# Second half of an RMSNorm: all eight multiplications moved to VectorE, read from the PSUM bank of the scale

## The chip, the cores and the metric

The kernel runs on one core of a Trainium2 chip. The time is device microseconds of one execution. Before the change it is 2491.94 us, the median of three runs (2489.65 to 2494.43). One further execution was profiled; all rows of the trace come from it. Engine names are those of the profile: PE is TensorE (PEld its weight loads), DVE is VectorE, ACT is ScalarE, POOL is GpSimd, SP the engine that issues the DMAs of the weights.

## What is computed

The reference is a trunk of two layers; x is 512 tokens by 1024 features in fp32. Each layer has three sub-layers, an FFN, a mixer and a second FFN, and every one begins with the same step:

```
def rms_norm(x, gain):
    xf = x.astype(jnp.float32)
    y = xf * lax.rsqrt(jnp.mean(xf * xf, axis=-1, keepdims=True) + EPS)
    return (y * gain.astype(jnp.float32)).astype(x.dtype)

h = modulate(rms_norm(x, norm_gain[l, i]), shift, scale)      # h * (1 + scale) + shift
x = x + 0.5 * gate * swiglu(h, w_gate, w_up, w_down)          # FFN
x = x + gate * hybrid_mixer(h, ...)                           # mixer
```

The norm at the head of a sub-layer stands between two stretches of matrix products: it needs the whole x that the last product of the sub-layer before it completes, and the first product of the next sub-layer needs its result h. There are six norms. The first is written apart, at the start of the program; the other five, at the seams between sub-layers, go through the class `Norm`, and the change is in that class alone.

## The kernel before

**Layout and precision.** x is kept transposed, features on the 128 partitions and tokens along the free axis, in eight slices d = 0 to 7 of 128 features, two slices to a tile. Products are made to fp32 precision from three matmuls: each operand is split into a high part and a low part (`hi`, the value rounded to fp32r, and `lo`, the rest), and lines 119, 120 and 121 multiply high by high and the two mixed pairs. So h exists as `hhi` and `hlo`, 8 slices of 128x512 each.

**The norm in two halves of tokens.** At a seam everything goes in two halves of 256 tokens (`hs` = 0 and 1), so that the first products on half 0 can run while half 1 is still being normalised. For a half there are these steps:
- `sq`, as each slice of x is completed (line 425 on DVE adds the product of the sub-layer before): ACT squares it (L314, for the last slice L319), POOL adds the square to `ssum` (L315; for the last slice DVE, L320, into the tile `strip`), and ACT writes the slice scaled by gain and 1 + scale into a tile `xa` (L323).
- `front`: PE adds the squares over the partitions (L332), DVE makes the inverse square root by Newton steps on 128x2 numbers (L334, L276, L282 to L284) and writes it on the diagonal of a 128x128 matrix, twice (L337, into `strip`).
- `back_start`: PE multiplies ones by the diagonals (L351). This leaves the scale of each token, repeated on all partitions, in a PSUM bank `rb` of 128x256. ACT copies the bank to the third part of `strip` (L353).
- eight pieces, one per slice d: a multiplication t = xa * scale, on DVE from the PSUM bank for d = 0, 3 and 6 (L360) and on POOL from the copy for d = 1, 2, 4, 5 and 7 (L362); then ACT adds the shift and rounds to `hhi` (L364), and DVE makes `hlo` = t + shift - hhi (L365).

**What consumes it.** In an FFN, PE takes slice after slice d: three matmuls of 256 tokens for the gate (`pg`) and three for the up projection (`pu`), then, for all eight slices, 24 for a second gate unit (`pg1`). In the mixer it takes six matmuls of 512 columns per slice, for the first six slices, out of weights fetched ahead (`ptb`, `b`). Half 1 follows in the same way.

**What sets the order.** Each engine carries out its own list of instructions in order and waits on semaphores for the others. The lists come from a scheduler in the tile library, which reorders what the program emits; the program itself delays pieces by a counter of matmuls (`later`, `poll`, `STEP`). The weights are loaded by SP, rounded to high parts on ACT (L268) and split on DVE (L270), well ahead of PE. `strip` is a tag with two buffers. PSUM has two tags of four banks, `mm` and `acc`; `rb` takes one of them in turn.

Of the kernel before, what the change touches and what calls it, by code (L numbers as in the profile page):

```python
# [15 lines left out]
F32 = mybir.dt.float32  # L16
# [3 lines left out]
ALU = mybir.AluOpType  # L20
AX = mybir.AxisListType

P = 128
# [17 lines left out]
def encoder_kernel(tc, xT, c, w_ada, b_ada, gains, w_gate, w_up, w_down, w_qkv, w_f, w_ubg,  # L41
                   qk_gain, rel, fbias, w_pool, pool_scale, w_branch, w_out, inv_cnt, w_first, out):
    nc = tc.nc
# [16 lines left out]
    def nm(s):  # L60
        uid[0] += 1
        return f"{s}_{uid[0]}"

    def st(shape, dt, tag, bufs):
        return sb.tile(shape, dt, tag=tag, bufs=bufs, name=nm(tag))
# [7 lines left out]
    def blk(tag, dt=F32R):  # L73
        bufs = {"xv": 4, "v2": 4, "b": NB}[tag]
        return st([P, 2, T], dt, tag, bufs)

    def t1(cols=T):
        return st([P, cols], F32, "t1", 2)
# [19 lines left out]
    def later(delay, fn, group=None):  # L98
        t = Task(pe[0] + delay, fn, group)
        tasks.append(t)  # L100
        return t
# [33 lines left out]
    for b in range(4):  # L135
        xb = blk("xv", F32)
        nc.sync.dma_start(xb, xT[:, 2 * b:2 * b + 2, :])
        x_blocks.append(xb)
        sq = st([P, 2, T], F32, "wlo" if b else "whi", 3)
        for a in range(2):  # L140
            nc.scalar.activation(sq[:, a, :], xb[:, a, :], AF.Square)
        squares.append(sq)
        if b < 2:
            pc = mmt()
            mm(pc, ones[0:1, :], crow[:, b * T:(b + 1) * T], start=True, stop=True)
            crows.append(pc)
# [141 lines left out]
    def xd(d):  # L288
        return x_blocks[d // 2][:, d % 2, :]

    HALF = T // 2


    class Norm:
# [10 lines left out]
        def sq(self, d, hs):  # L305

            cols = slice(0, T) if hs is None else slice(hs * HALF, (hs + 1) * HALF)
            x = xd(d)[:, cols]
            n = cols.stop - cols.start
            if d == 0:  # L310
                nc.scalar.activation(self.ssum[:, cols], x, AF.Square)
            elif d < KD - 1:
                q = t1(T)[:, :n]
                nc.scalar.activation(q, x, AF.Square)  # L314
                nc.gpsimd.tensor_tensor(self.ssum[:, cols], self.ssum[:, cols], q, op=ALU.add)  # L315
            else:
                self.work[hs] = st([P, 3 * HALF], F32, "strip", 2)
                w = self.work[hs][:, :HALF]
                nc.scalar.activation(w, x, AF.Square)  # L319
                nc.vector.tensor_tensor(w, w, self.ssum[:, cols], op=ALU.add)  # L320
            if d % 2 == 0 and self.xa[d // 2] is None:
                self.xa[d // 2] = blk(self.xtag, F32)
            nc.scalar.activation(self.xa[d // 2][:, d % 2, cols], x, AF.Identity, scale=apre[:, self.l, self.s, d:d + 1])  # L323
# [20 lines left out]
        def back_start(self, hs, bank):  # L344
            if self.state[hs] > 1:
                return
            self.front(hs, bank)
            self.state[hs] = 2
            w = self.work[hs]
            rb = bank((P, HALF))  # L350
            mm(rb, ones, w[:, HALF:2 * HALF], start=True, stop=True)  # L351
            rbs = w[:, 2 * HALF:3 * HALF]
            nc.scalar.copy(rbs, rb)  # L353
            cols = slice(hs * HALF, (hs + 1) * HALF)

            def piece(d):
                b = modc[:, self.l, 3 * self.s, d:d + 1]
                t = self.xa[d // 2][:, d % 2, cols]
                if d in ON_DVE:
                    nc.vector.tensor_tensor(t, rb, t, op=ALU.mult)  # L360
                else:
                    nc.gpsimd.tensor_tensor(t, rbs, t, op=ALU.mult)  # L362
                hi = hhi[:, d, cols]
                a_ins = nc.scalar.activation(hi, t, AF.Identity, bias=b)  # L364
                v_ins = nc.vector.scalar_tensor_tensor(hlo[:, d, cols], t, b, hi.bitcast(F32),  # L365
                                                       op0=ALU.add, op1=ALU.subtract)
                gate["scalar"], gate["vector"] = a_ins.ins, v_ins.ins
                last["norm"] = v_ins.ins

            self.pieces[hs] = [lambda d=d: piece(d) for d in range(KD)]  # L370
            for d in range(KD):
                later(STEP * d, lambda d=d: self.pieces[hs].pop(0)() if len(self.pieces[hs]) == KD - d else None)
# [59 lines left out]
    FRONT, BACK, FRONT1, BACK1 = 8, 24, 16, 28  # L432
    FRONT2, BACK2 = 16, 28
    STEP = 3
    ON_DVE = (0, 3, 6)


    class Ffn:
# [205 lines left out]
    def proj_qk(l, col, gcol, is_q, res, pre=None, norm=None):  # L644
# [3 lines left out]
        def evac(t, a):  # L648
            if t == 0:
                qs.extend((st([P, NT, T], F32, "ptb", 2), st([P, NT, H], F32, "qss", 1)))  # L650
            qn, ss = qs
            nc.scalar.copy(qn[:, t, :], a)
            sq = t2(T)
            nc.scalar.activation(sq, a, AF.Square)  # L654
            nc.vector.tensor_reduce(ss[:, t, :], sq.rearrange("p (h d) -> p h d", h=H), axis=AX.X, op=ALU.add)
# [441 lines left out]
```

## Time and profile before

| | before |
|---|---|
| median of 3 runs | 2491.94 us (2489.65 to 2494.43) |
| the profiled execution | 2496.94 us, its span in the trace 2495.0 us |
| PE busy | 2429.8 us, 97% of the span, 11898 matmuls |
| DVE busy | 1378.6 us, 55% |
| ACT busy | 983.6 us, 39% |
| POOL busy | 380.7 us, 15% |
| the copy of the scale (L353) | 10 times, 373 ns median |
| multiplications on DVE from PSUM (L360) | 30, medians 414 to 416 ns |
| multiplications on POOL from the copy (L362) | 50, medians 741 and 914 ns |

The row of a timeline gives the start in us, the duration in us (of all instructions of the row together, where it ends in xN), engine, line, operation, out<-in and shape, and in brackets the idle time of the engine just before and what ended it. Matmuls are pipelined, so a row's duration is longer than the distance to the next row; the distance is what PE needs for one. PEclk in a row of stretches is the TensorE clock that was granted, 1.00 being full speed.

### The profile page before, as it was taken

The numbers are of one execution on the slowest core, as the hardware profiler recorded it, in microseconds if no ns is written. First come the engines' busy times: TensorE is split into PE (matmuls) and PEld (weight loads), VectorE is DVE, ScalarE is ACT, GpSimd is POOL, SyncE is SP. The second block draws the span as 40 slices with busy tenths as digits, with TensorE's granted clock in tenths as the row PEclk, the third lists the DMA queues.
The fourth block names the chain that finished last, engine by engine and source line by source line (L and its number), as shares of the span: only waits on it lengthen the run. The fifth ranks groups of instructions, "written<-read, shape, count | busy, mean of one in ns | idle before, by whom it ended". The sixth has DMA issues, their size and how long they took to land. (4 is left out here: it accounts for less than half of the span.)

```text
span 2495.0 us, 30866 instructions
## 1 busy us (share of the span) xinstructions
PE 2429.8 (97%) x11898; PEld 2030.3 (81%) x11898; DVE 1378.6 (55%) x2424; ACT 983.6 (39%) x1644; POOL 380.7 (15%) x377
## 2 busy tenths in 40 slices
PE   7999999989999999999999999999999999999999
PEld 5888888767788898888888888977777888888888
DVE  8655536788753465555365543467787434533332
ACT  5322235677532442223333222356765334422231
POOL 2000003343322220000110000124332322100000
PEclk9999999999999999999999999999999999999999
DMA  7655542223323425555335533323233233232322
GB/s 276 224 186 199 180 141 80 85 72 96 104 89 110 146 99 193 178 207 181 119 114 191 190 114 99 126 78 92 67 105 99 93 115 130 69 101 93 102 93 93
DMA packets 116263, 320.02 MB, mean 128 GB/s; under 512 B 11122, under 2 KB 13298, under 8 KB 116116
## 3 DMA queue, kind: packets, MB, share of 16 engines
q1 hardware_dynamic: 114962, 313.86, 37.3%
q0 software_dynamic: 1152, 4.19, 0.4%
q8 instruction: 93, 1.52, 0.2%
q14 instruction: 54, 0.44, 0.1%
q10 hardware_dynamic: 2, 0.00, 0.0%
HBM read 311.64 MB, written 6.38 MB: 127 GB/s over the span
## 5 line engine op out<-in xcount | busy, mean ns | idle before, releaser
L268 ACT CAST whi<-raw 128x1024 fp32r<-128x1024 f32 (+1 forms) x395 | 411.8, 1046 | 1090.9 <-PE acc L120 416.7
L270 DVE TENSOR_TENSOR wlo<-raw,whi 128x1024 fp32r<-128x1024 f32 x339 | 419.1, 1239 | 519.5 <-ACT whi L268 507.5
L121 PE MATMUL mm<-hhi,wlo 128*128 128x512 f32 x1304 | 507.4, 389 | 0.4 <-DVE wlo L270 0.4
L119 PE MATMUL mm<-hhi,whi 128*128 128x512 f32 x1304 | 507.6, 389 | 0.0
L120 PE MATMUL mm<-hlo,whi 128*128 128x512 f32 x1304 | 507.3, 389 | 0.0
L119 PE MATMUL acc<-b,whi 128*128 128x512 f32 (+1 forms) x960 | 355.9, 371 | 0.0
L121 PE MATMUL acc<-b,wlo 128*128 128x512 f32 (+1 forms) x960 | 353.4, 368 | 0.0
L120 PE MATMUL acc<-b,whi 128*128 128x512 f32 (+1 forms) x960 | 353.4, 368 | 0.0
L121 PEld LDWEIGHTS mm<-hhi,wlo 128*128 128x128 f32 x1304 | 244.7, 188 | 51.5 <-DVE wlo L270 0.9
L119 PEld LDWEIGHTS mm<-hhi,whi 128*128 128x128 f32 x1304 | 245.1, 188 | 50.8
L120 PEld LDWEIGHTS mm<-hlo,whi 128*128 128x128 f32 x1304 | 244.8, 188 | 50.9
L197 DVE CUSTOM_DVE_ANT_0 v<-v,b,badac 128x1024 f32<-128x1024 f32 x144 | 189.3, 1316 | 40.3 <-DMA v<-in_w_ada_dram 40.0
L121 PEld LDWEIGHTS acc<-b,wlo 128*128 128x128 f32 x960 | 180.9, 188 | 29.6
L120 PEld LDWEIGHTS acc<-b,whi 128*128 128x128 f32 x960 | 181.0, 189 | 29.3 <-DVE b L376 0.3
L119 PEld LDWEIGHTS acc<-b,whi 128*128 128x128 f32 x960 | 181.0, 189 | 28.8
L119 PE MATMUL acc<-hhi,whi 128*128 128x512 f32 x480 | 191.7, 401 | 1.7 <-ACT hhi L564 1.7
L120 PE MATMUL acc<-hlo,whi 128*128 128x512 f32 x480 | 188.5, 393 | 1.1 <-DVE hlo L567 1.1
L121 PE MATMUL acc<-hhi,wlo 128*128 128x512 f32 x480 | 188.9, 393 | 0.5 <-POOL wlo L270 0.4
L462 DVE TENSOR_TENSOR t<-mm,t 128x512 f32<-128x512 f32 x86 | 59.5, 691 | 210.0 <-PE mm L121 205.9
L270 POOL TENSOR_TENSOR wlo<-raw,whi 128x1024 fp32r<-128x1024 f32 (+1 forms) x56 | 132.5, 2370 | 172.1 <-ACT whi L268 137.3
L119 PE MATMUL acc<-whi,hhi 128*128 128x512 f32 x336 | 137.6, 409 | 4.9 <-ACT t L654 3.7
L120 PE MATMUL acc<-wlo,hhi 128*128 128x512 f32 x336 | 131.8, 392 | 0.0
(235 smaller groups left out, 3473.3 us busy)
## 6 DMA issues: line engine op xcount, KB each, us to landing
v<-in_w_ada_dram SPq DMA_DIRECT2D x144, 512.0 KB, 4.5
raw<-in_w_down_dram SPq DMA_DIRECT2D x88, 512.0 KB, 3.7
raw<-in_w_up_dram SPq DMA_DIRECT2D x82, 512.0 KB, 3.5
raw<-in_w_gate_dram SPq DMA_DIRECT2D x79, 512.0 KB, 3.5
raw<-in_w_ubg_dram SPq DMA_DIRECT2D x56, 512.0 KB, 3.5
raw<-in_w_qkv_dram SPq DMA_DIRECT2D x42, 512.0 KB, 3.6
raw<-in_w_branch_dram SPq DMA_DIRECT2D x24, 512.0 KB, 3.7
raw<-in_w_out_dram SPq DMA_DIRECT2D x16, 512.0 KB, 3.6
```

The lines of the kernel that those rows point to most:

```text
L119: mm(o, lh, rh, start=start, stop=False)
L120: mm(o, lh, rl, start=False, stop=False)
L121: mm(o, ll, rh, start=False, stop=stop)
L197: dot = nc.vector.tensor_tensor_reduce(out=raw, in0=raw, in1=silc[0], scale=1.0, scalar=badac[:, l, j, d:d + 1], op0=ALU.mult, op1=ALU.add ...
L268: nc.scalar.copy(hi, raw)
L270: lo_eng.tensor_tensor(lo, raw, hi.bitcast(F32), op=ALU.subtract)
L462: nc.vector.tensor_tensor(pr, pu, sg, op=ALU.mult)
```

## The change

The multiplication of every piece goes to DVE and reads the scale from its PSUM bank. The copy of the bank on ACT and the third part of `strip` go away; POOL has no part in the second half of the norm any more. The bank `rb` is read until the multiplication of piece 7, where before it was last read by the copy and the pieces 0, 3 and 6.

```
@@ Norm.sq
-                self.work[hs] = st([P, 3 * HALF], F32, "strip", 2)
+                self.work[hs] = st([P, 2 * HALF], F32, "strip", 2)
@@ Norm.back_start
             mm(rb, ones, w[:, HALF:2 * HALF], start=True, stop=True)
-            rbs = w[:, 2 * HALF:3 * HALF]
-            nc.scalar.copy(rbs, rb)
             cols = slice(hs * HALF, (hs + 1) * HALF)

             def piece(d):
                 b = modc[:, self.l, 3 * self.s, d:d + 1]
                 t = self.xa[d // 2][:, d % 2, cols]
-                if d in ON_DVE:
-                    nc.vector.tensor_tensor(t, rb, t, op=ALU.mult)
-                else:
-                    nc.gpsimd.tensor_tensor(t, rbs, t, op=ALU.mult)
+                nc.vector.tensor_tensor(t, rb, t, op=ALU.mult)
                 hi = hhi[:, d, cols]
                 a_ins = nc.scalar.activation(hi, t, AF.Identity, bias=b)
@@
     STEP = 3
-    ON_DVE = (0, 3, 6)
```

The changed program is six lines shorter, so its lines are renumbered: L360 (multiplication) becomes L357, L364 (`hhi`) L359, L365 (`hlo`) L360, L376 L371, L425 L420. The scheduler also sets the lists differently at the five seams. Three places matter.

**DVE, half 0 of the norm ahead of the first mixer.** `v_422` is the tile of slices 0 and 1, `v_425` of 2 and 3, `v_458` of 4 and 5, `v_461` of 6 and 7; `mm_2871` is the bank of the scale. Before:

```order
L360 TENSOR_TENSOR v_422_2488<-mm_2871,v_422_2488 128x256 [waits Activation_49]
L360 TENSOR_TENSOR v_425_2523<-mm_2871,v_425_2523 128x256
L360 TENSOR_TENSOR v_461_2767<-mm_2871,v_461_2767 128x256
L365 SCALAR_TENSOR_TENSOR hlo<-v_422_2488,modc,hhi 128x256 [waits Activation_49]
L425 SCALAR_TENSOR_TENSOR xv_97<-acc_2548,modc,xv_97 128x256 [waits PE_49]
L365 SCALAR_TENSOR_TENSOR hlo<-v_425_2523,modc,hhi 128x256 [waits Activation_49]
```

Now:

```order
L357 TENSOR_TENSOR v_422_2488<-mm_2871,v_422_2488 128x256 [waits PE_49]
L357 TENSOR_TENSOR v_422_2488<-mm_2871,v_422_2488 128x256
L357 TENSOR_TENSOR v_425_2523<-mm_2871,v_425_2523 128x256 x2
L360 SCALAR_TENSOR_TENSOR hlo<-v_422_2488,modc,hhi 128x256 [waits Activation_49] x2
L420 SCALAR_TENSOR_TENSOR xv_97<-acc_2548,modc,xv_97 128x256 [waits PE_49]
L360 SCALAR_TENSOR_TENSOR hlo<-v_425_2523,modc,hhi 128x256 [waits Activation_49] x2
L420 SCALAR_TENSOR_TENSOR xv_97<-acc_2549,modc,xv_97 128x256 [waits PE_49]
L357 TENSOR_TENSOR v_458_2732<-mm_2871,v_458_2732 128x256 x2
```

The first multiplication waits for PE instead of the copy on ACT, and four multiplications stand ahead of the first `hlo` where three stood.

**ACT, half 1 of the same norm.** Before, with the copy of the scale first:

```order
L353 COPY strip_2916<-mm_2997 128x256 [waits PE_49]
L364 ACTIVATE hhi<-v_422_2488,modc 128x256 [waits Pool_49]
L364 ACTIVATE hhi<-v_422_2488,modc 128x256 [waits DVE_49]
L364 ACTIVATE hhi<-v_425_2523,modc 128x256 [waits Pool_49]
L364 ACTIVATE hhi<-v_425_2523,modc 128x256 [waits DVE_49]
```

Now:

```order
L359 ACTIVATE hhi<-v_422_2488,modc 128x256 [waits DVE_49] x2
L359 ACTIVATE hhi<-v_425_2523,modc 128x256 [waits DVE_49] x2
L359 ACTIVATE hhi<-v_458_2732,modc 128x256 [waits DVE_49] x2
L359 ACTIVATE hhi<-v_461_2767,modc 128x256 [waits DVE_49] x2
```

Before, slice 1, which POOL multiplies, was rounded ahead of slice 0; now the slices go in their order.

**DVE, the inverse square root of half 1, same norm.** Before, all of half 0's `hlo` stood ahead of L334, the first step of it. Now one multiplication and one `hlo` (slice 7 of half 0) stand around and inside it:

```order
L357 TENSOR_TENSOR v_461_2767<-mm_2871,v_461_2767 128x256
L334 TENSOR_SCALAR nt_v_2960<-mm_2957 128x2 [waits PE_49]
L371 TENSOR_TENSOR ssum_4753<-wf_4751,ssum_4753 128x8x8 [waits Activation_49]
L276 TENSOR_SCALAR nt_j_2962<-nt_v_2960 128x2 [waits DVE_49]
L282 TENSOR_TENSOR nt_q_2964<-nt_j_2962 128x2 [waits DVE_49]
L283 SCALAR_TENSOR_TENSOR nt_u_2965<-nt_q_2964,nt_v_2960 128x2 [waits DVE_49]
L360 SCALAR_TENSOR_TENSOR hlo<-v_461_2767,modc,hhi 128x256 [waits Activation_49]
L284 SCALAR_TENSOR_TENSOR nt_z_2966<-nt_u_2965,nt_j_2962 128x2 [waits DVE_49]
```

The other four seams have the same pattern (without L371 in the FFNs). In PE's list L351 of half 1 moves back by one matmul at the mixers and by two at the FFNs, where L332 of half 1 moves ahead by seven.

More of the change, by code (lines that the diff above doesn't have):

```diff
@@ L316, in sq @@
             else:
-                self.work[hs] = st([P, 3 * HALF], F32, "strip", 2)
+                self.work[hs] = st([P, 2 * HALF], F32, "strip", 2)
                 w = self.work[hs][:, :HALF]
@@ L351, in back_start @@
             mm(rb, ones, w[:, HALF:2 * HALF], start=True, stop=True)
-            rbs = w[:, 2 * HALF:3 * HALF]
-            nc.scalar.copy(rbs, rb)
             cols = slice(hs * HALF, (hs + 1) * HALF)
@@ L358, in piece @@
                 t = self.xa[d // 2][:, d % 2, cols]
[L359 to L362, printed above, removed]
+                nc.vector.tensor_tensor(t, rb, t, op=ALU.mult)
                 hi = hhi[:, d, cols]
@@ L434, in encoder_kernel @@
     STEP = 3
-    ON_DVE = (0, 3, 6)
     class Ffn:
```

## The prediction

> **What bounds the kernel now.** I read the page first, then the stretches, the waits of PE, and the timeline of each seam.
>
> ```profile
> span 2495.0 us, 30866 instructions
> PE 2429.8 (97%) x11898; PEld 2030.3 (81%) x11898; DVE 1378.6 (55%) x2424; ACT 983.6 (39%) x1644; POOL 380.7 (15%) x377
> PE acc L121 <- DVE hlo L365: 4.3, 2, 2.2
> PE acc L119 <- ACT hhi L364: 1.7, 2, 0.8
> PE mm L119 <- ACT hhi L364: 1.3, 3, 0.4
> PE mm L120 <- DVE hlo L365: 1.1, 3, 0.4
> PE acc L332 <- DVE strip L320: 0.7, 3, 0.2
> ```
>
> PE bounds the program, so a change in the norm is worth what it takes from PE at the five seams, and nothing else. The waits (us in total, times, longest) that PE has on the norm's second half come to 4.3 + 1.7 + 1.3 + 1.1 + 0.7 = 9.1 us, two at each mixer seam and three at each FFN seam. They are not the whole loss. The timeline of PE at the first mixer:
>
> ```profile
> 387.40 0.40 PE L119 MATMUL acc<-ptb,hhi 128*128 128x512 f32 x1
> 387.63 0.40 PE L120 MATMUL acc<-ptb,hhi 128*128 128x512 f32 x1
> 390.19 0.61 PE L121 MATMUL acc<-ptb,hlo 128*128 128x512 f32 x1 [2.16 <-DVE hlo L365]
> 390.59 0.63 PE L119 MATMUL acc<-ptb,hhi 128*128 128x512 f32 x1
> 393.94 0.39 PE L121 MATMUL acc<-ptb,hlo 128*128 128x512 f32 x1
> 394.16 0.39 PE L119 MATMUL acc<-ptb,hhi 128*128 128x512 f32 x1
> 395.56 0.50 PE L332 MATMUL mm<-ones,strip 128*128 128x1 f32 x4
> 398.79 0.70 PE L351 MATMUL mm<-strip,ones 128*128 128x256 f32 x2
> 400.48 0.40 PE L121 MATMUL acc<-b,hlo 128*128 128x512 f32 x1
> 401.71 0.50 PE L119 MATMUL acc<-ptb,hhi 128*128 128x512 f32 x1 [0.83 <-ACT hhi L364]
> 390.19:393.94 3.75, 3.75 (x10) 2.96 (x10) 3.69 (x10) 3.27 (x9) 1.77 (x4) 0.54 0.49 156
> ```
>
> An unhindered matmul of 512 columns follows the one before it after 0.23 us. From 387.63 to 390.19 it took 2.56: 2.33 lost. Then nine matmuls took 3.75 us where 9 x 0.23 = 2.1 were due, and the last row (a stretch; the third number from its end is the granted clock) says why: the clock stood at 0.54. That is 1.6 more, of which I count 1.5. Half 1 loses 401.71 - 400.48 - 0.23 = 1.0, and 0.1 in the matmul after it. So a first mixer seam loses 3.8 in half 0 and 1.1 in half 1. The second mixer seam has the same two waits and, read in the same way, loses 4.0 and 1.1:
>
> ```profile
> 1625.07 0.50 PE L121 MATMUL acc<-ptb,hlo 128*128 128x512 f32 x1 [2.16 <-DVE hlo L365]
> 1636.60 0.50 PE L119 MATMUL acc<-ptb,hhi 128*128 128x512 f32 x1 [0.83 <-ACT hhi L364]
> ```
>
> Together 10.0 us.
>
> What made `hlo` late there, on DVE, POOL and ACT:
>
> ```profile
> 385.13 1.09 DVE L360 TENSOR_TENSOR v<-mm,v 128x256 f32<-128x256 f32 x3 [0.35 <-ACT strip L353]
> 386.25 3.88 DVE L365 SCALAR_TENSOR_TENSOR hlo<-v,modc,hhi 128x256 fp32r<-128x256 f32 x1
> 386.38 3.46 POOL L362 TENSOR_TENSOR v<-strip,v 128x256 f32<-128x256 f32 x5
> 393.00 1.28 DVE L365 SCALAR_TENSOR_TENSOR hlo<-v,modc,hhi 128x256 fp32r<-128x256 f32 x3
> 399.93 1.09 DVE L360 TENSOR_TENSOR v<-mm,v 128x256 f32<-128x256 f32 x3 [1.20 <-ACT strip L353]
> 401.29 4.71 DVE L365 SCALAR_TENSOR_TENSOR hlo<-v,modc,hhi 128x256 fp32r<-128x256 f32 x8 [0.28 <-ACT hhi L364]
> 399.98 4.15 POOL L362 TENSOR_TENSOR v<-strip,v 128x256 f32<-128x256 f32 x5 [6.54 <-ACT strip L353]
> 384.73 0.37 ACT L353 COPY strip<-mm 128x256 f32<-128x256 f32 x1 [0.17 <-PE mm L351]
> 399.52 0.37 ACT L353 COPY strip<-mm 128x256 f32<-128x256 f32 x1 [5.63 <-PE mm L351]
> 400.75 2.17 ACT L364 ACTIVATE hhi<-v,modc 128x256 fp32r<-128x256 f32 x5 [0.85 <-POOL v L362]
> ```
>
> One `hlo`, an operation with both tensors in SBUF, lasted 3.88 us; POOL's five multiplications ran from 386.38 to 389.84, and DVE came free 0.3 us behind them. Three `hlo` with POOL quiet (393.00) take 1.28, so 0.48 one and 0.40 from one to the next. Beside POOL's multiplications (401.29) eight take 4.71, 0.6 from one to the next. The multiplications on DVE, which read one tensor from PSUM, keep 0.34 from one to the next beside POOL. So POOL's multiplications hold up DVE's `hlo`, but not DVE's multiplications. The Trainium skill, page "SBUF — State Buffer", section "Who interferes with whom", states just that: an instruction of DVE with two SBUF inputs contends with one of GpSimd that reads SBUF, the one that starts first blocking the other, and one with at most one SBUF input does not. By that rule the new multiplications are free of it and the old contention ends; the rows agree.
>
> The third thing in these rows: in half 1 ACT waits for POOL (400.75), whose product of slice 1 stands in ACT's list ahead of slice 0. PE's first `hhi` is the second one ACT writes.
>
> An FFN seam, whose units of work on PE are 0.12 us (256 columns):
>
> ```profile
> 891.35 0.28 PE L119 MATMUL mm<-hhi,ptb 128*128 128x256 f32 x1
> ...
> 895.56 0.28 PE L121 MATMUL mm<-hhi,ptb 128*128 128x256 f32 x1
> 896.06 0.61 PE L332 MATMUL acc<-ones,strip 128*128 128x1 f32 x4 [0.22 <-DVE strip L320]
> 899.46 0.64 PE L351 MATMUL acc<-strip,ones 128*128 128x256 f32 x2
> 901.60 0.28 PE L121 MATMUL mm<-hhi,b 128*128 128x256 f32 x1
> 902.32 0.50 PE L119 MATMUL mm<-hhi,ptb 128*128 128x256 f32 x2 [0.44 <-ACT hhi L364]
> 902.66 0.28 PE L119 MATMUL mm<-hhi,b 128*128 128x256 f32 x1
> 903.32 0.38 PE L120 MATMUL mm<-hlo,ptb 128*128 128x256 f32 x1 [0.38 <-DVE hlo L365]
> 903.55 0.28 PE L121 MATMUL mm<-hhi,ptb 128*128 128x256 f32 x1
> ```
>
> Half 0 loses 896.06 - 895.56 - 0.12 = 0.4 at L332 and, ahead of it, some 0.4 in five delays of about 0.1 at `hlo` (read one by one from the timeline). Half 1: from 901.60 to 903.55 five matmuls took 1.95 where 5 x 0.12 = 0.6 were due, 1.35. In all 2.15; the two other FFN seams read the same. Three times 2.15 is 6.5, so the most that can be won is 10.0 + 6.5 = 16.5 us.
>
> **The change part by part.**
>
> The copy: 10 times 0.37 off ACT. It stood on the path of every half: DVE began 0.40 behind ACT's start (399.93 against 399.52, 385.13 against 384.73), so a half's first product comes 0.4 earlier, 0.7 behind the start of L351.
>
> The five multiplications a half that move: POOL loses 50 of about 0.8; DVE gains 50 x 0.34 = 17 us. DVE's share of the program does not matter (55%); its list within a seam does. A piece now costs DVE 0.34 + 0.40 = 0.74 and ACT 0.40 to 0.45. PE needs six matmuls a slice: 1.40 us at a mixer, 0.71 at an FFN. So a mixer is safe, and at an FFN DVE is 0.03 slower a slice, 0.2 in a half, within the lead that it has there.
>
> *Mixer, half 0.* In the written order, with the times of the old rows: first multiplications at 384.73, 385.07, 385.40, 385.74; ACT rounds slice 0 from 385.6 to 386.1 (the two older instructions L314 and L323 first); `hlo` 0 at 386.2, or 386.4 if POOL's one sum (L315) holds it, 1 at 386.8, then a residual (L425, 0.4), 2 and 3 by 388.5, the next residual, then slices 4 and 5 with `hlo` at 390.3 to 391.1. PE asks for `hlo` d at 387.86 + 1.40 d, so for 4 at 393.5. Nothing is late. The 3.8 (4.0) goes, the slow clock with it, since the gap ahead of it goes.
>
> *Mixer, half 1.* Here the change adds a wait. Before, L351 began 3.23 us behind L332, just as DVE's chain ended. Now an `hlo` (0.40) stands in the chain, and PE has one more matmul (0.23): a new wait of 0.2, up to 0.4 if L371 also takes a place. Behind L351 come five matmuls, until 1.7 us behind its start; slice 0 is multiplied at 0.7, rounded from 1.25 to 1.75. A wait of 0.1 in place of 1.0. Half 1 keeps 0.3 to 0.5 of its 1.1: I take 0.5. Gain of a mixer seam 3.8 + 0.6 = 4.4 (4.6 the second): 9.0 us.
>
> *FFN, half 0.* In the same way `hlo` 4, the first behind both residuals, is done at about 894.5. PE begins slice 0 at 891.35 and, 24 matmuls on, slice 4 at 894.2; L332 is now ahead of `hlo` 4 in PE's list, at 894.4, with its input (L320) done by 893.6, so PE asks for `hlo` 4 at 895.1. `hlo` 7, inside the inverse root, ends at 896.7, asked for at 897.3. The chain has 33 matmuls of cover (3.9 us and 0.5 for L332 itself) where 24 stood, and needs 3.4 + 0.4: no wait. The 0.8 goes, or 0.1 stays.
>
> *FFN, half 1.* 13 matmuls stay behind L351, so PE asks for slice 0 at 2.0 us behind its start and has it at 1.75; for `hlo` 0 at 2.25, there at 2.3; `hlo` 6 is within 0.1. About 0.2 stays of 1.35. Gain of an FFN seam 1.9, three times 5.7.
>
> Nothing else pays. `rb` is held some 6 us longer, but the next tile that takes its bank comes a unit of work later. The splits of weights that follow (L270) begin up to 1 us later relative to PE; the first of them is needed 11.4 us behind L351 and is there by 9.
>
> Sum: 9.0 + 5.7 = 14.7 us, of at most 16.5. The profiled execution goes from a span of 2495.0 to 2480.3; it took 2496.94, 1.9 around the span and 5.0 over the median. The median 2491.94 goes to 2477.2; I say 2478, with a wait or two overlooked.
>
> **Unknown costs.** A DVE list with two multiplications between `hlo`s is not in the trace. From below it keeps the 0.34 and 0.40; from above `hlo` keeps the 0.6 of row 401.29 for another reason than POOL. I take the first, by row 393.00, which differs from it in POOL alone. The wait at L351 lies between 0 and 0.4 at a mixer. Whether PE's gain passes through to the end: PE's list of waits names no DMA, so what follows moves with PE; at worst it is all absorbed.
>
> **The rivals.**
>
> *Only the mixers win (2483).* The FFN seams run on units of 0.71 a slice with a lead of a few tenths; if DVE's order makes one `hlo` late in each half, waits of the old size come back. Against it, the order above. 9.0 us remain.
>
> *The long `hlo` stays (2486).* If 3.88 us were not POOL's doing, the mixers would win 0.6 each and the FFNs as forecast, 6 us in all. Against it: its end follows POOL's fifth multiplication.
>
> *Absorbed (2492).* PE comes early at the end of a seam and waits for something that does not move. For it: attention between the seams has PE waits of its own. Against it: they are on DVE and ACT, which are fed by PE.
>
> *Slower: DVE becomes the bound of the FFN halves (2498).* If `hlo` stays at 0.6 from one to the next, a piece costs 0.94 against PE's 0.71: 8 x 0.23 = 1.8 a half, 11 in six halves. If each FFN seam also brings one slow spell of the clock (1.5, as at 390.19), 4.5 more. The FFNs' old loss of 6.5 stays; less the mixers' 9.0 the time grows by 6.5. It decides from an `hlo` distance of 0.56 on (48 x 0.19 = 9.0). Against it: row 393.00. The Trainium skill, page "TensorE: Matmul & The Clock Gate", section "What's actually happening", puts the half clock behind an idle window of about 3.4 us; the row at 390.19 has it behind 2.16 us of idle already, so the row decides. By the page, short waits at the FFNs would bring no slow spell and this rival would end at 2494.
>
> **How the numbers follow.** Forecast 0.62, only the mixers 0.17, long `hlo` stays 0.06, absorbed 0.09, slower 0.06. The forecast's own range is 2474 to 2482: from the whole 16.5 and a lower draw (the three runs lie within 2.5 of their median) to 11 us of gain with a higher one. To hold 8 in 10 it is carried on over the first rival and its spread: 2473 to 2486. A measurement tells about 0.2%, 5 us, from no change. Faster than 2487: the first two, the most of the third: 0.83. Within 0.2%: absorbed and the rest of the third, 0.11. Slower 0.06.
>
> **What would show it.** No `hlo` over 1 us; eight in half 1 of a seam 0.40 apart; full clock at both mixer seams; PE without a wait over 0.5 there; ACT's first `hhi` of half 1 1.25 behind L351 instead of 1.96; a small wait of PE at L351 of the mixers' half 1. It is wrong if PE's wait on `hlo` appears at later slices of the FFN halves, if `hlo` stays long, or if the seams get shorter and the span does not.

## The result and the profile after

The changed kernel takes 2479.69 us, the median of five runs (2475.76 to 2481.9), where the kernel before, in five runs beside it, takes 2491.94. The ratio is 0.9948 with a 95% interval of 0.9937 to 0.996, so 10 to 16 us are won. Its profiled execution took 2480.69 us. The page of it begins:

```profile
span 2478.9 us, 30855 instructions
PE 2425.1 (98%) x11898; PEld 2030.1 (82%) x11898; DVE 1372.2 (55%) x2474; ACT 979.9 (40%) x1634; POOL 340.5 (14%) x327
```

POOL has 50 instructions fewer and DVE 50 more, and yet DVE is busy 6 us less: the multiplications add 17 us (50 x 0.34), the `hlo` that no longer wait beside POOL take 18 away (53.4 us busy before, 35.0 now), and the rest of the 6 lies outside the norm. Of the five rows of PE's waits that were shown of before (9.1 us in all), none is left in the list of after: no entry names `hlo` or `hhi` of the norm (L360, L359), or `strip` from L320.

The first mixer seam in the timeline of after, on PE, DVE and ACT (start, duration, then as before; multiplication is now L357, `hhi` L359, `hlo` L360):

```profile
388.66 0.40 PE L120 MATMUL acc<-ptb,hhi 128*128 128x512 f32 x1
388.89 0.39 PE L121 MATMUL acc<-ptb,hlo 128*128 128x512 f32 x1
...
392.63 0.50 PE L332 MATMUL mm<-ones,strip 128*128 128x1 f32 x4
...
396.14 0.70 PE L351 MATMUL mm<-strip,ones 128*128 128x256 f32 x2
...
397.59 0.39 PE L121 MATMUL acc<-b,hlo 128*128 128x512 f32 x1
397.89 0.50 PE L119 MATMUL acc<-ptb,hhi 128*128 128x512 f32 x1
385.75 1.42 DVE L357 TENSOR_TENSOR v<-mm,v 128x256 f32<-128x256 f32 x4
387.15 0.98 DVE L360 SCALAR_TENSOR_TENSOR hlo<-v,modc,hhi 128x256 fp32r<-128x256 f32 x2
...
396.87 1.08 DVE L357 TENSOR_TENSOR v<-mm,v 128x256 f32<-128x256 f32 x3 [0.79 <-PE mm L351]
397.88 1.29 DVE L360 SCALAR_TENSOR_TENSOR hlo<-v,modc,hhi 128x256 fp32r<-128x256 f32 x3
399.08 1.08 DVE L357 TENSOR_TENSOR v<-mm,v 128x256 f32<-128x256 f32 x3
397.33 1.31 ACT L359 ACTIVATE hhi<-v,modc 128x256 fp32r<-128x256 f32 x3 [4.16 <-DVE v L357]
```

PE goes from L120 to the first `hlo` product in 0.23 us where it needed 2.56. Two `hlo` take 0.98 in half 0 instead of 3.88 for one. In half 1, DVE does three multiplications, three `hlo`, three multiplications: 399.08 - 396.87 = 2.21 for three pieces, 0.74 a piece. ACT's first `hhi` starts 1.19 behind L351 (1.96 before), and PE's first product of half 1 comes 0.30 behind the matmul ahead of it, 0.07 more than it needs. The stretch that held the slow clock before now reads (third number from the end is the granted clock):

```profile
388.40:391.40 3.00, 3.00 (x15) 2.45 (x14) 3.00 (x9) 2.47 (x7) 1.75 (x4) 1.00 0.31 127
```

The first FFN seam, on PE:

```profile
891.04 0.40 PE L119 MATMUL mm<-hhi,ptb 128*128 128x256 f32 x2
891.27 0.50 PE L332 MATMUL acc<-ones,strip 128*128 128x1 f32 x4
...
895.63 0.59 PE L351 MATMUL acc<-strip,ones 128*128 128x256 f32 x2
...
897.49 0.28 PE L121 MATMUL mm<-hhi,b 128*128 128x256 f32 x1
897.61 0.40 PE L119 MATMUL mm<-hhi,ptb 128*128 128x256 f32 x2
897.84 0.35 PE L120 MATMUL mm<-hlo,ptb 128*128 128x256 f32 x1
898.03 0.28 PE L121 MATMUL mm<-hhi,ptb 128*128 128x256 f32 x1
```

L332 no longer waits, and half 1 begins 0.12 behind the last matmul of half 0, the distance that a matmul of 256 columns needs.

For all kernels below I use one measure, the length of a seam on PE: from L351 of half 0 to the first matmul with weights behind the seam that are not fetched ahead. PE has the same matmuls in it in all of them, so a difference is time that PE lost.

| kernel | mixer seams, us | FFN seams, us | sum of five | against after | median, us | ratio to the runs of before beside it (95%) |
|---|---|---|---|---|---|---|
| before | 26.12, 26.12 | 23.57, 23.58, 23.56 | 122.95 | +16.6 | 2491.94 | 1 |
| after | 21.21, 21.21 | 21.33, 21.33, 21.29 | 106.37 | 0 | 2479.69 | 0.9948 (0.9937 to 0.996) |
| before, again | 26.14, 24.59 | 23.58, 23.57, 23.59 | 121.47 | +15.1 | 2493.26 | 1.0001 (0.9992 to 1.0009) |
| before, a third time | 26.14, 24.60 | 23.58, 23.60, 23.59 | 121.51 | +15.1 | 2491.18, one run | |
| after, again | 21.23, 21.22 | 21.33, 21.33, 21.30 | 106.41 | 0 | 2479.07 | 0.9943 (0.9931 to 0.9956) |
| after, POOL reads | 23.41, 23.41 | 22.69, 22.70, 22.70 | 114.91 | +8.5 | 2490.26 | 0.9986 (0.9977 to 0.9995) |
| after, POOL writes | 21.30, 21.29 | 21.33, 21.33, 21.33 | 106.58 | +0.2 | 2478.35 | 0.9953 (0.9936 to 0.997) |
| after, a copy nobody reads | 21.94, 21.94 | 21.96, 21.94, 21.95 | 109.73 | +3.4 | 2482.84 | 0.9959 (0.9947 to 0.9972) |
| after, DVE reads the copy | 22.02, 22.03 | 22.66, 22.66, 22.66 | 112.03 | +5.7 | 2484.99 | 0.9968 (0.9955 to 0.998) |
| before, two slices on POOL | 23.14, 23.12 | 22.97, 22.93, 22.94 | 115.10 | +8.7 | 2487.27 | 0.9977 (0.9968 to 0.9986) |
| after, every product twice | 24.42, 24.41 | 25.31, 25.61, 25.61 | 125.36 | +19.0 | 2500.56 | 1.0034 (1.0021 to 1.0047) |

The stretches of the FFNs between the seams are 341.9 us in all these traces; those with attention lie between 475.0 and 479.4 from one execution to the next, whichever kernel runs. That is why one profile can be some us off its median.

### The profile page after: what moved, and what is told of

Read it like the earlier page. It is cut to its first block, busy times and chain, and to the rows that moved or that the text cites. A ratio compares the mean times of both kernels' runs of the same rounds, so it can differ in the third digit from the quotient of the medians.

```text
span 2478.9 us, 30855 instructions
## 1 busy us (share of the span) xinstructions
PE 2425.1 (98%) x11898; PEld 2030.1 (82%) x11898; DVE 1372.2 (55%) x2474; ACT 979.9 (40%) x1634; POOL 340.5 (14%) x327
## 3 DMA queue, kind: packets, MB, share of 16 engines
q8 instruction: 93, 1.52, 0.3%
## 5 line engine op out<-in xcount | busy, mean ns | idle before, releaser
L120 PE MATMUL mm<-hlo,whi 128*128 128x512 f32 x1304 | 507.3, 389 | 0.0
L120 PE MATMUL acc<-b,whi 128*128 128x512 f32 (+1 forms) x960 | 353.4, 368 | 0.0
L120 PEld LDWEIGHTS mm<-hlo,whi 128*128 128x128 f32 x1304 | 244.8, 188 | 50.8
L120 PEld LDWEIGHTS acc<-b,whi 128*128 128x128 f32 x960 | 181.1, 189 | 29.3 <-DVE b L371 0.3
L120 PE MATMUL acc<-hlo,whi 128*128 128x512 f32 x480 | 188.9, 394 | 1.0 <-DVE hlo L561 1.0
L120 PE MATMUL acc<-wlo,hhi 128*128 128x512 f32 x336 | 132.3, 394 | 0.0
```

The source lines that it names most:

```text
L120: mm(o, lh, rl, start=False, stop=False)
```

## Experiments

My theory: the gain is the end of POOL's reading of SBUF beside DVE's `hlo`, plus the copy (0.4 on the path of each half) and ACT's list, which no longer puts POOL's product first. The rivals: the gain comes from the copy, or from the other order of the lists that the scheduler sets, or POOL is late for its own sake and PE waits for its products.

### POOL reads SBUF, and nobody waits for it

In the changed kernel, behind the multiplication of slice 0 of each half, POOL gets five products that no instruction reads. The norm is computed as in the changed kernel, and PE's matmuls stand in the same order.

```
                nc.vector.tensor_tensor(t, rb, t, op=ALU.mult)
+               if d == 0:
+                   for o in (w[:, 2 * HALF:], w[:, :HALF], w[:, HALF:2 * HALF], self.ssum[:, cols], w[:, 2 * HALF:]):
+                       nc.gpsimd.tensor_tensor(o, t, t, op=ALU.mult)
```

> The changed kernel with five extra multiplications on GpSimd in each half, t * t of slice 0 into memory that nobody reads, so that GpSimd is as busy at that place as before but nobody waits for its products; the lists of PE, DVE and ACT are those of the changed kernel but for a few rows. Theory 1a (contention: GpSimd's reads of SBUF hold up DVE's hlo): hlo lasts 2 to 4 us once in half 0 of each mixer seam, hlo of half 1 are 0.6 apart, the seams lose 2 to 5 us each at the mixers and 1 to 2 at the FFNs, time 2487 to 2492. Theory 1b (only the lateness and the order of GpSimd's products mattered): hlo stays at 0.48 us, the time stays at 2480.

Measured: 2490.26 us, ratio 0.9986 (0.9977 to 0.9995); the seams are 8.5 us longer than in after. The first mixer seam, in the timeline of this kernel (the products that nobody reads are L360, `hlo` is L363):

```profile
385.91 3.81 DVE L363 SCALAR_TENSOR_TENSOR hlo<-v,modc,hhi 128x256 fp32r<-128x256 f32 x2
386.15 1.75 POOL L360 TENSOR_TENSOR strip<-v 128x256 f32<-128x256 f32 x3
387.87 0.60 POOL L360 TENSOR_TENSOR ssum<-v 128x256 f32<-128x256 f32 x1
388.44 0.60 POOL L360 TENSOR_TENSOR strip<-v 128x256 f32<-128x256 f32 x1
389.38 0.50 PE L121 MATMUL acc<-ptb,hlo 128*128 128x512 f32 x1 [1.57 <-DVE hlo L363]
398.33 2.20 POOL L360 TENSOR_TENSOR strip<-v 128x256 f32<-128x256 f32 x3 [5.97 <-DVE v L357]
398.83 1.99 DVE L363 SCALAR_TENSOR_TENSOR hlo<-v,modc,hhi 128x256 fp32r<-128x256 f32 x3
```

The old picture is back with work that nobody waits for. The row of two `hlo` takes 3.81 us; less 0.40 for the second, the first one lasts 3.4, until 0.3 behind the end of POOL's fifth product at 389.04, and PE waits. In half 1 three `hlo` take 1.99 instead of 1.29. So POOL's reading alone takes back more than half of the seams' gain (8.5 of 15.1 to 16.6) and three quarters of the medians' (by the ratios 0.0014 is left of 0.0055), with the copy gone and the products of the norm all on DVE. Behind this shorter wait the clock stayed whole:

```profile
389.00:394.00 5.00, 4.62 (x22) 3.85 (x23) 5.00 (x14) 2.84 (x7) 1.60 (x4) 1.00 0.42 155
```

PE's list is that of after, matmul for matmul; ACT's and DVE's differ from it in the place of one instruction at each mixer seam. So if the parts simply add up, the rivals "the copy" and "the lists" cannot be more than the rest; "POOL late for its own sake" has no share in these 8.5 us.

### POOL as an engine that only writes

The same place, but twelve memsets in place of the five products.

```
+               if d == 0:
+                   for i in range(3):
+                       for o in (w[:, HALF:2 * HALF], w[:, :HALF], self.ssum[:, cols], w[:, 2 * HALF:]):
+                           nc.gpsimd.memset(o, 0.0)
```

> The changed kernel, and in each half, behind the multiplication of slice 0, POOL gets twelve memsets of 128x256 that nobody reads: POOL is as long busy as with the five products of the run before it, about 3.5 us a half, but only writes SBUF and reads nothing. The computation is whole. Theory (what holds hlo up is that POOL reads SBUF while DVE reads two tensors from SBUF): hlo stays at 0.40 from one to the next, no wait of PE on hlo at the mixers, the seams sum to 106.4 to 107.5 us, and the time is that of the changed kernel, 2479 to 2481. Rival (any work of POOL beside hlo, or POOL's writes to SBUF, holds it up): hlo of several us in the mixers' half 0 as with the five products, seams near 115, time 2488 to 2491. A third, between: memsets hold only the hlo that meets the write of one of them, then hlo 0.5 to 0.6 apart in half 1, seams 108 to 111, time 2482 to 2485.

Measured: 2478.35 us, seams 106.58. The first mixer seam in this kernel's timeline (memsets L361, `hlo` L364):

```profile
385.56 0.76 POOL L315 TENSOR_TENSOR ssum<-ssum,t 128x256 f32<-128x256 f32 x1
385.93 1.08 DVE L364 SCALAR_TENSOR_TENSOR hlo<-v,modc,hhi 128x256 fp32r<-128x256 f32 x2
386.24 0.70 POOL L361 MEMSET strip<- 128x256 f32 x2
...
389.64 1.04 POOL L361 MEMSET ssum<- 128x256 f32 x3 [0.19 <-DVE strip L320]
389.87 1.29 DVE L364 SCALAR_TENSOR_TENSOR hlo<-v,modc,hhi 128x256 fp32r<-128x256 f32 x3
```

Three `hlo` beside three memsets take 1.29, as with POOL quiet (1.28 in the row at 393.00 of before, 1.29 in after). The test is weaker than I meant: the scheduler spread the memsets, so POOL has no burst of 3.5 us beside the first `hlo`. But the first `hlo` of half 0 begins here as it does in the run with POOL's reads, while POOL works on its sum (L315, which reads), and memsets follow where products followed there: the first two `hlo` take 1.08 instead of 3.81. The 20 `hlo` of this kernel that overlap memsets of the experiment and no sum take 0.47 to 0.49 each, while one that begins early in a product of POOL takes 0.83 in that run. POOL's reads do it, not POOL's work as such. The Trainium skill, page "SBUF — State Buffer", section "Who interferes with whom", says the same of a GpSimd instruction that only writes, and these rows agree.

### The copy alone

The changed kernel with the copy put back on ACT; nothing reads it.

```
+           rbs = w[:, 2 * HALF:3 * HALF]
+           nc.scalar.copy(rbs, rb)
```

> The changed kernel with the copy of the scale made on ACT as before, but read by nobody; the first multiplication on DVE again stands behind it in the scheduler's list. It prices the copy alone. If the copy is on the path: each half's first product 0.4 later, covered in half 0, felt in half 1: seams 0.3 to 0.4 longer each, 1 to 2 us in all, time about 2481. If it is hidden: 2479.7. If the copy was the main gain: 2486 or more.

Measured: 2482.84 us, ratio 0.9959 (0.9947 to 0.9972), seams 3.4 us longer, 0.7 a seam, twice what I expected. First mixer seam, half 1 (copy L353, multiplication L359, `hhi` L361):

```profile
395.18 0.60 PE L351 MATMUL mm<-strip,ones 128*128 128x256 f32 x2
...
396.08 0.40 PE L121 MATMUL acc<-b,hlo 128*128 128x512 f32 x1
397.24 0.50 PE L119 MATMUL acc<-ptb,hhi 128*128 128x512 f32 x1 [0.77 <-ACT hhi L361]
396.22 1.08 DVE L359 TENSOR_TENSOR v<-mm,v 128x256 f32<-128x256 f32 x3 [1.39 <-ACT strip L353]
```

DVE's first product waits for the copy although it does not read it: it begins 1.04 behind L351 where it began 0.73 behind in after, since its wait in the list is on ACT. The loss is larger than that, 397.24 - 396.08 - 0.23 = 0.9: only three matmuls stand between L351 and the first product of half 1, where five stand in after. The scheduler set L351 two matmuls later, and 2 x 0.23 = 0.47 of cover went with it. Between them, 0.3 to 0.4 by the start and 0.5 by the list, the 0.9 is accounted for. In half 0 nothing is lost. So a part of what "removing the copy" brought came by the list that the scheduler makes without it; this run cannot give the two apart in microseconds of the whole.

### DVE multiplies from the copy

The changed kernel with the copy, and all eight multiplications, on DVE still, reading it, so that both operands are in SBUF.

```
+           rbs = w[:, 2 * HALF:3 * HALF]
+           nc.scalar.copy(rbs, rb)
-               nc.vector.tensor_tensor(t, rb, t, op=ALU.mult)
+               nc.vector.tensor_tensor(t, rbs, t, op=ALU.mult)
```

> The changed kernel with the copy of the scale put back on ACT and all eight multiplications on DVE reading that copy: GpSimd is out, the copy is in. Theory 1 (the gain is GpSimd's absence: its reads held up hlo, and its products came late and out of order): most of the gain stays; half 1 starts 0.4 later, which costs 0.4 at each mixer seam and 0.2 to 0.4 at each FFN seam, 1.5 to 2 us, time about 2481.5. Theory 2 (the gain is the copy's absence from the path): the gain goes, 2488 to 2492.

Measured: 2484.99 us, ratio 0.9968 (0.9955 to 0.998), seams 5.7 us longer than after and 2.3 longer than with the copy that nobody reads. First mixer seam (multiplication L359):

```profile
384.85 1.97 DVE L359 TENSOR_TENSOR v<-strip,v 128x256 f32<-128x256 f32 x4 [0.35 <-ACT strip L353]
385.38 0.82 POOL L315 TENSOR_TENSOR ssum<-ssum,t 128x256 f32<-128x256 f32 x1
```

Four multiplications that take 1.42 from PSUM take 1.97 from SBUF, beside one sum of squares on POOL that was there all along. Further on, with POOL quiet, they keep 0.34 apart as from PSUM. So the bank as a source frees the multiplications from POOL, besides saving the copy. What that is worth is not shown by itself: the mixers, of which these rows are, pay 0.1 each (22.02 against 21.94), and the 2.3 are the FFNs', 0.7 each, where four multiplications beside a sum also take 1.98 (at 886.31), but where PE's list differs too. The median lies between the two theories, 3.5 us above the first and 3 below the second: neither holds alone. Still, somewhat more than half of the gain remains here: 0.0032 of 0.0055 by the ratios, taking 0.9945 between the two of after.

### Half-way: two slices on POOL

The kernel before with its copy, and POOL left with slices 5 and 7.

```
-    ON_DVE = (0, 3, 6)
+    ON_DVE = (0, 1, 2, 3, 4, 6)
```

> The kernel before with GpSimd left only slices 5 and 7 of the multiplications; the copy of the scale stays. It undoes most of the old arrangement but keeps the mechanism. If contention is proportional to GpSimd's reads, hlo is held up by up to two multiplications (1.5 us) instead of five, PE's wait on hlo in half 0 of the mixers goes since slices 5 and 7 come late, and what is left is the copy: seams as with the dead copy, 110 us together, plus up to 1 us each in half 1, time 2483 to 2486. If any GpSimd multiplication is as bad as five: 2490.

Measured: 2487.27 us, ratio 0.9977 (0.9968 to 0.9986), seams 8.7 us over after. The seams are as expected, the median is 1 us above the range. First mixer seam (multiplication on POOL L362, `hhi` L364, `hlo` L365):

```profile
387.64 2.26 DVE L365 SCALAR_TENSOR_TENSOR hlo<-v,modc,hhi 128x256 fp32r<-128x256 f32 x2
387.77 1.44 POOL L362 TENSOR_TENSOR v<-strip,v 128x256 f32<-128x256 f32 x2
...
399.23 2.51 ACT L364 ACTIVATE hhi<-v,modc 128x256 fp32r<-128x256 f32 x6 [0.85 <-POOL v L362]
400.19 0.50 PE L119 MATMUL acc<-ptb,hhi 128*128 128x512 f32 x1 [1.07 <-ACT hhi L364]
```

The length of the long `hlo` follows the length of POOL's run: 3.88 with five products, and 1.86 (the row of two, less 0.40) with two. The second pair of rows is the other part of the theory. The scheduler puts POOL's slice at the head of ACT's list in half 1 again, and PE waits 1.07 for it. A dose between gives a gain between, but not in proportion: three of five products moved, and less than half of the gain came.

### Every product twice on DVE

How much room has DVE? In the changed kernel every multiplication is made twice, first into a strip that nobody reads.

```
+               nc.vector.tensor_tensor(junk, rb, t, op=ALU.mult)
                nc.vector.tensor_tensor(t, rb, t, op=ALU.mult)
```

> The changed kernel with every multiplication made twice on VectorE, once into memory that nobody reads: a piece costs VectorE 1.08 us instead of 0.74. It measures how near VectorE is to being the bound of the seams, the rival of the prediction that ended slower. PE takes 0.71 us for a slice at an FFN and 1.40 at a mixer. If the prediction's count holds, the FFN halves become VectorE's: 8 x 0.37 less a lead of 0.3 is 2.7 us a half, 16 in six halves, the FFN seams some 26.5 us instead of 21.3, the mixer seams under 1 us longer, time about 2497. If VectorE had room to spare the time stays near 2480.

Measured: 2500.56 us, ratio 1.0034 (1.0021 to 1.0047). A piece now costs DVE 0.74 + 0.34 = 1.08, more than PE's 0.71 at an FFN. The first FFN seam in its timeline (two rows), the first mixer seam (two rows), and the stretches behind the last wait in the three FFN seams and in the first mixer seam:

```profile
900.58 0.70 PE L351 MATMUL acc<-strip,ones 128*128 128x256 f32 x2 [0.39 <-DVE strip L337]
902.79 0.79 PE L119 MATMUL mm<-hhi,ptb 128*128 128x256 f32 x2 [1.52 <-ACT hhi L361]
397.64 0.70 PE L351 MATMUL mm<-strip,ones 128*128 128x256 f32 x2 [1.47 <-DVE strip L337]
399.86 0.50 PE L119 MATMUL acc<-ptb,hhi 128*128 128x512 f32 x1 [1.52 <-ACT hhi L361]
```

```profile
903.40:906.40 3.00, 3.00 (x16) 3.00 (x16) 2.97 (x9) 1.15 (x3) 0.00 (x0) 0.53 0.00 0
1270.60:1273.60 3.00, 2.98 (x18) 2.96 (x18) 2.97 (x9) 1.15 (x3) 0.00 (x0) 0.64 0.00 0
2140.70:2143.70 3.00, 2.98 (x19) 2.98 (x19) 2.97 (x9) 1.14 (x3) 0.00 (x0) 0.69 0.00 0
400.40:403.40 3.00, 3.00 (x14) 2.42 (x13) 2.97 (x10) 1.23 (x3) 0.00 (x0) 1.00 0.00 0
```

The FFN seams grow by 4.0 to 4.3, of which about 0.9 to 1.4 is the slow clock (an estimate: 3 us of each stretch, less its granted share). The mixers, which I had held for safe, grow by 3.2 each: there, in half 1, L351 waits 1.47 and the first `hhi` 1.52. A piece of 1.08 is less than PE's 1.40 at a mixer, but DVE's list holds more than pieces: in the first mixer seam L334 starts at 391.94 and the next step of the inverse root (L276) at 394.14, with four products and two `hlo` in between. So eight more multiplications a half cost 19 us of seams, where the five that the change moved cost at most about 0.1, and the rival that DVE becomes the bound is a real mechanism: the change itself stays just below it.

### The two kernels again

The kernel before unchanged, twice, and the changed one unchanged.

> The kernel before, unchanged, profiled a second time. In the two profiles the five seams together got 16.6 us shorter, while the medians differ by 12.25. If the slow spell of the clock behind the 2.16 us wait is the same in every execution, this profile shows 26.1 us from one L351 to the next weights at both mixer seams and 23.6 at the FFN seams again, and the missing 4 us lie elsewhere. If the spell is a matter of chance, at least one mixer seam shows the full clock and some 24.6 us instead of 26.1. Time 2490 to 2495, ratio 1.00 either way.

> The kernel before, profiled a third time, for two more mixer seams. Of four so far three had a slow spell of the clock behind the wait of 2.16 us (26.1 us from L351 to the next weights) and one had none (24.6). If the spell is chance, each of the two seams shows one of these two lengths; a third length, or a wait other than 2.16, would speak against it.

> The changed kernel again, on the chip and beside the runs of the kernel before that the other experiments of this call have. Expected 2479.7, ratio 0.9948, seams together 106.4 us as in its first profile, full clock at both mixer seams; since no wait there is over 0.1 us, no chance is left in the seams.

Measured: 2493.26, 2491.18 (one run) and 2479.07 us. The seams of the changed kernel repeat within 0.02 us. Those of the kernel before don't: the second mixer seam is 26.12 in the first profile and 24.59 and 24.60 in the two others. The stretches of the first repetition that hold the two waits on `hlo`:

```profile
387.20:394.00 6.80, 4.64 (x15) 3.34 (x13) 6.74 (x11) 3.56 (x10) 4.25 (x8) 0.75 0.31 107
1621.40:1629.00 7.60, 5.44 (x27) 4.18 (x26) 7.32 (x15) 3.54 (x10) 4.23 (x8) 1.00 0.28 106
```

The wait on `hlo` is there both times (4.3 us in two, as before), the slow clock only behind the first. Of six mixer seams in three profiles of the kernel before, four have the spell and two have not (the first seam has it in all three profiles, the second in one), and it costs 1.5 us where it comes.

## Why the prediction was right, and where its sum was off

**What bounds.** Right. PE's waits on the second half of the norm are gone and the span follows: the seams are 16.6 us shorter and the span 16.1. The rival *absorbed* is out.

**Long `hlo` is POOL's doing.** Right, and shown: reading products that nobody waits for bring it back, and memsets in their place don't. The rival *the long `hlo` stays* is out.

**DVE's list.** "From below it keeps the 0.34 and 0.40" held: 0.74 a piece, where the upper bound was 0.94. The 0.6 of row 401.29, from which that bound came, is a mean of two paces: while POOL works, until 404.13, `hlo` start up to 0.88 apart (401.69, 402.58, 403.46), and then 0.40. The rival in which DVE becomes the bound of the FFN halves did not come about, with its threshold of 0.56 for `hlo` far off; the run with every product twice shows the mechanism at work from a piece of 1.08 on.

**Mixer, half 0.** The 3.8 went as said (3.9 by L351 to L351: 14.69 to 11.02, with one matmul of 0.23 more ahead of L351 now). Mis-sized was "the slow clock with it": 1.5 a seam was counted as always there, and it is there in four of six. By these six, a seam of the kernel before loses on average 1.0 by it, so that the two seams of a usual run had about 1 us less to win than I counted.

**Mixer, half 1.** The step that failed in size is "a new wait of 0.2, up to 0.4" at L351 and "I take 0.5" for what stays. From L332 to L351 it is 3.51 now and was 3.23: the chain grew by 0.28, not by a whole `hlo` of 0.40 and more, since that `hlo` fills a gap between two of the small steps. In the timeline of after:

```profile
393.76 0.16 DVE L283 SCALAR_TENSOR_TENSOR nt_u<-nt_q,nt_v 128x2 f32<-128x2 f32 x1
393.84 0.48 DVE L360 SCALAR_TENSOR_TENSOR hlo<-v,modc,hhi 128x256 fp32r<-128x256 f32 x1
394.24 0.15 DVE L284 SCALAR_TENSOR_TENSOR nt_z<-nt_u,nt_j 128x2 f32<-128x2 f32 x1
...
394.62 0.16 DVE L283 SCALAR_TENSOR_TENSOR nt_u<-nt_q,nt_v 128x2 f32<-128x2 f32 x1
394.82 0.16 DVE L284 SCALAR_TENSOR_TENSOR nt_z<-nt_u,nt_z 128x2 f32<-128x2 f32 x1
```

From L283 to L284 it is 0.48 with the `hlo` between and 0.20 without, 0.28 more. One more matmul on PE covers 0.23 of that, and 0.05 is left. About 0.1 stayed of 1.1, and the seam gained 4.9 where 4.4 and 4.6 were forecast.

**FFN.** Half 0 without a wait, as worked out. In half 1 "about 0.2 stays" was 0.07 (897.84 to the next matmul at 898.03, where 0.12 was due), and a seam gained 2.24 to 2.27 instead of 1.9; that is a little more than the 2.15 that I had read as its whole loss. The rival *only the mixers win* is out: the three FFN seams gave 6.8 us, against 5.7.

**The copy.** "0.4 on the path of each half" is what the run with the copy alone shows at the start of the chain, but what it costs is 0.7 a seam, since the scheduler's list changes with it. The order of PE's list around L351 was read for the change itself, so this does not touch the sum.

**The sum.** 14.7 was forecast and 16.6 came in the profiles (2478.9 for a span forecast at 2480.3). In the medians it is 12.3 here, and 13.8 in the second comparison (2492.9 for the kernel before there, 2479.07), against a forecast of 14. Two errors of opposite sign lie in it: 1.9 too little at the seams, and the slow spells, counted in full. That the median came within 2 us of the forecast is in part luck. With the spells at 2.0 instead of 3.0, the seams give 15.6, inside the interval of the ratio (10 to 15.7 us), at its upper end. The remaining 2 to 3 us are open: six seams are few to count spells by (with no spell at all the seams would give 13.6), and outside the seams the three profiles of before take 2367.7 to 2372.1 us and the two of after 2370.9 and 2372.5, a spread larger than what is missing.

**Where the gain comes from.** POOL's reading gives 8.5 us of seams when put back alone, the copy 3.4 (the change of the lists that comes with it included), 11.9 of 15.1 to 16.6 together. The rest, 3 to 5, was not measured by itself; the wait for POOL's product at the head of ACT's list (0.83 at each mixer, 1.07 in the half-way kernel) and the spells of the clock, which the run with POOL's reads has not, are what is seen in the rows.

## What to carry to other kernels

When two engines share a chain of small SBUF operations, look at the duration of each instruction beside its neighbours: one that lasts eight times its usual time (here 3.88 us for 0.48) is being held up, and the work to move may be that of the neighbour, even if nobody waits for it. Moving work onto the busier engine can pay if it is done there from another source (here a PSUM bank, 0.34 a piece, free of the contention) and the new list still fits under the consumer's time for a piece; work that out at the tightest consumer (0.74 against 0.71 with a lead held, 1.08 against 0.71 without), and count the other work in the same list (at 1.08 the mixers lost 3.2 us too, against a consumer's 1.40). A removed instruction is also removed from the scheduler's list, so compare the lists and not only the path.

## What the hardware showed that I had not expected

**A whole run of products holds one `hlo`, or only one at a time.** In half 0 of a mixer the `hlo` that meets POOL's run is done only when the last of POOL's products is (3.88 us with five, 1.86 with two), while POOL goes on undisturbed, a product every 0.57 us in the run with POOL's reads and every 0.69 in before. In half 1, with the same instructions on both engines, they take turns and both are slower: in before one `hlo` and one product come about every 0.88, in the run with POOL's reads about every 0.76. The Trainium skill, page "SBUF — State Buffer", section "Who interferes with whom", has the instruction that starts first block the other for its own length. The taking of turns is near to that, though a turn is shorter than the two alone (0.40 + 0.69 = 1.09 and 0.40 + 0.57 = 0.97); a block that lasts over a run of five does not fit it. What decides between the two is open. In all six cases of the long block the `hlo` began in the last 0.3 us of POOL's sum L315, with products right behind it; but at an FFN of before an `hlo` that began 0.3 ahead of the end of a product, with another right behind (892.06), took only 0.57.

**The slow clock does not go by the length of the wait alone.** Behind one wait of 2.16 us: four times of six. Behind one of 1.57, with POOL reading: not in two. Behind 0.39 and 1.52 with L351 between them, at the FFN seams with every product twice: three times of three, at 0.53, 0.64 and 0.69 over the stretch. Behind 1.47 and 1.52 at the two mixers of that kernel: not. The Trainium skill, page "TensorE: Matmul & The Clock Gate", section "What's actually happening", describes a window of about 3.4 us that runs freely and doesn't start with the kernel's work; that the same wait shows both outcomes agrees with a window that runs freely, while idle times well below its length already bring the slow clock here.
